# Partial sums of a two-level block multiply: gate in one ScalarE function, running sums kept in one PSUM bank

## Chip, cores and metric

The kernel runs on one core of a Trainium2 chip. The metric is the device time of one execution in microseconds (us); lower is better. The engines have these names in the profile: PE is TensorE (matrix products), PEld its loading of weights, DVE is VectorE, ACT is ScalarE, POOL is GpSimd, SP is SyncE.

## The reference

One layer of a streaming encoder on `x` of shape (1, 1024, 1024) in float32: a mixer (short convolution and forgetting attention) and then a dense SwiGLU block, each between two RMS norms. What the change touches is the first half of the SwiGLU block:

```python
def swiglu(h, w_gate_up, w_down):                  # h: (1, 1024, 1024)
    gu = jnp.einsum("bsd,df->bsf", h, w_gate_up)   # w_gate_up: (1024, 2 * 2816)
    g, u = jnp.split(gu, 2, axis=-1)
    return jnp.einsum("bsf,fd->bsd", jax.nn.silu(g) * u, w_down)
```

## The kernel before

The whole kernel is one core's program: projections, attention, merge and output projection, then the SwiGLU block with its gate_up product and its down product. All large products are done in two float32r parts: an operand is converted into a high part (`hi`, by ScalarE) and a remainder (`lo`, by VectorE), and `mm3` multiplies high by high, high by low and low by high.

**Blocks.** The hidden width 2816 is cut into 22 blocks of 128 columns (`NF`), numbered 0 to 21. A block needs its gate `g` and its `u` for 1024 rows, each held as two halves of 128 x 512. Gate and up are treated as the two block rows of a Strassen-Winograd multiply: instead of eight products there are seven, of the combinations A11, A12, S1, S2, S3, S4, A22 of weights with B11, B21, T1, T2, T3, B22, T4 of activations. One product (`prod`) is 12 matmuls of 128x128 weights with a 128x512 moving operand, accumulated in one PSUM bank; there are eight banks, handed out in turn (`bank`). The results are sums of products: gate left = A11 + A12, gate right (`c12`) = A11 + S2 + S1 + S4, up right (`c22`) = A11 + S2 + S1 + S3, up left = A11 + S2 + S3 + A22, where each name stands for its product.

**Three stretches of gate_up.** For blocks 0 to 10 (`NPRE` = 11) A11 and A12 are done earlier; their results `p1` and `g1` are kept or go through DRAM (`pre_dram`). The *rest loop* does the other five products of each of these, through `strassen(...)`, in the order S2, S1, S3, S4, A22. Block 11 (`lone`) goes through the same function with all seven. Blocks 12 to 21 go in five pairs (x, y) through `two_blocks`, where the fourth product is itself done one level deeper for the pair together (`prod2` into `zb` and into the `b3` banks).

**Order.** Instructions are listed per engine by a planner, which takes the earlier-written one first where it may choose and works with its own estimates of durations. `strict[0]` names engines on which the written order holds. It is `("tensor",)` inside `two_blocks`, so TensorE's order there is the written one; in the rest loop it is empty.

**Weights.** `prep_first` and `prep_rest` load and convert the weights of one block. The buffers rotate: four for `hi`, three for `lo`. A buffer is written again only when every reader of its earlier tile is done. In the pairs each block takes three `lo` tiles, in this order: one for A11 and A12, one (`lx`) for S2 and S3, one (`l2`) for S1 and A22. In the rest loop a block takes two, `lx` and `l2`.

```python
def hi_t():
    return wtile("hi", 4, F32R)
def lo_t():
    return wtile("lo", 3, F32R)
...
S2=(hx[:, LO], lx[:, LO]), S3=(hx[:, UP], lx[:, UP]),
S1=(h2[:, LO], l2[:, LO]), A22=(h2[:, UP], l2[:, UP]),
...
nc.tensor.matmul(ps, ah, bh, start=start, stop=False, **kw)
nc.tensor.matmul(ps, ah, bl, start=False, stop=False, **kw)
nc.tensor.matmul(ps, al, bh, start=False, stop=stop, **kw)
```

Here `a` is the weight operand and `b` the activation, so `lo` of the weights is first read by a product's third matmul and last by its twelfth.

Every engine instruction is recorded under one line (L77, the helper that passes it on), so instructions are told apart by tile: `lo<-raw,hi` is the conversion that fills an `l2` tile or that of A11 and A12, `lo<-sx,hi` that of an `lx`, `b` a PSUM bank, `c` and `um` the float32 sums in SBUF, `sgf` the sigmoid's result.

Of the kernel before, what the change touches and what calls it, by code (L numbers as in the profile page):

```python
# [12 lines left out]
AF = mybir.ActivationFunctionType  # L13
# [9 lines left out]
NC = 512  # L23
# [16 lines left out]
NPRE = 11  # L40


B11, B21, B22, T1, T2, T3, T4 = range(7)
A11, A12, A22, S2, S3, S4, S1 = range(7)
# [3 lines left out]
def block_kernel(  # L48
# [16 lines left out]
    n1, n2 = slice(0, NC), slice(NC, S)  # L65
# [3 lines left out]
    class InOrder:  # L69


        def __init__(self, name):
            self.name, self.engine = name, getattr(bass_nc, name)
# [11 lines left out]
    nc = SimpleNamespace(  # L85
        **{e: InOrder(e) for e in engines}
    )
# [7 lines left out]
    def pool(name, bufs=1, side="left", space=None):  # L95
        kw = dict(name=name, bufs=bufs)
        if space is not DRAM:
            kw["reuse_waits"] = "tile"
        if space is not None:
            kw["space"] = space  # L100
        else:
            kw["side"] = side
        stack = ExitStack()
        ctx.callback(stack.close)
        return stack.enter_context(tc.tile_pool(**kw)), stack.close
# [4 lines left out]
    def add(o, a, b):  # L110
        nc.vector.tensor_tensor(o, a, b, op=ALU.add)
# [4 lines left out]
    def mul(o, a, b):  # L116
        nc.vector.tensor_tensor(o, a, b, op=ALU.mult)
# [11 lines left out]
    def copy(o, a):  # L129
        nc.scalar.activation(o, a, AF.Copy)  # L130
# [6 lines left out]
    def mm3(ps, a, b, start, stop, **kw):  # L137

        ah, al = a
        bh, bl = b  # L140
# [4 lines that stand above are left out]
    cpool, _ = pool("const")  # L145
    stat, _ = pool("stat", 4, side="right")
    stat.tile([P, 56], F32, name="pad", bufs=1)
    dpool, _ = pool("dram", space=DRAM)
# [10 lines left out]
    pre_dram = [dpool.tile([2, P, NC], F32, name=f"pre_dram{f}") for f in range(NPRE)]  # L159
# [52 lines left out]
    def z_tile(name, dt=F32, w=S):  # L212
        return zp.tile([P, S], dt, tag="z", name=name, bufs=2)[:, :w]
# [286 lines left out]
    for st in range(2, ST):  # L500
        ops, rest = cur
# [31 lines left out]
    wpool, _ = pool("w")  # L533
# [80 lines left out]
    def bank(psp, name):  # L614
        return psp.tile([P, NC], F32, tag="mm", name=name)

    def prod(ps, w, b, first):
        (ah, al), (bh, bl) = w, b
        kw = {} if first else dict(skip_group_check=True)
        for k in range(4):  # L620
            mm3(
                ps,
                (ah[:, k, :], al[:, k, :]),
                (bh[:, k, :], bl[:, k, :]),
                first and k == 0,
                k == 3,
                **kw,
            )

    def t_(tmp, name):  # L630
        return tmp.tile([P, NC], F32, tag=name, name=name)
# [11 lines left out]
    def strassen(w, hb, psp, tmp, p1=None, mid=None):  # L643

        b1 = None
        if p1 is None:
            b1 = bank(psp, "b1")
            prod(b1, w["A11"], hb[B11], True)
            p1 = t_(tmp, "c21")
            copy(p1, b1)  # L650
        b2, b3 = bank(psp, "b2"), bank(psp, "b3")
        prod(b2, w["S2"], hb[T2], True)
        c12 = t_(tmp, "c12")
        add(c12, p1, b2)
        prod(b3, w["S1"], hb[T1], True)
        c22 = t_(tmp, "c22")
        add(c22, p1, b3)
        if b1 is not None:
            prod(b1, w["A12"], hb[B21], False)
        prod(b2, w["S3"], hb[T3], False)  # L660
        add(c22, c22, b2)
        if mid is not None:
            mid()
        prod(b3, w["S4"], hb[B22], False)
        add(c12, c12, b3)
        prod(b2, w["A22"], hb[T4], False)
        c21 = p1
        add(c21, p1, b2)
        return b1, c12, c21, c22
# [20 lines left out]
    psm, psm_close = pool("psm", 6, space=PSUM)  # L690

    def wcols(c0):
        return win[:, c0 : c0 + P]
# [352 lines left out]
    for ij, (kind, j, _, _) in enumerate(jobs):  # L1046
        work = side.pop(ij, [])

        def mid():
            for cut, _ in work:  # L1050
                pinned(cut, "vector", "scalar")
# [7 lines left out]
        if ij < 2:  # L1059
# [15 lines left out]
            w = {**w, **prep_rest(wcols(jobs[ij][3]), r1)}  # L1075
            if ij == 1:
                pairs.q.append(pairs.prep(*pairs.srcs.popleft()))
            _, c12, c21, c22 = strassen(w, h1b, psm, pp, p1, mid)
        elif ij < len(jobs) - 1:
# [3 lines left out]
            w = pairs.get()  # L1083
            if ij in (12, 13):
                cb_of(0, ij - 12)
            c11, c12, c21, c22 = strassen(w, h1b, psm, pp, None, mid)
        else:
            w = pairs.get()
# [3 lines left out]
            c11, c12, c21, c22 = last_pair(w)  # L1092
# [91 lines left out]
    was, sgs = {}, {}  # L1184
# [173 lines left out]
    for t in range(2, NU + 2):  # L1358
        turned = None
        now = groups(t) if t < NU else ([], [])  # L1360
# [17 lines left out]
        if t == NU:  # L1378
            lasts = []
            for e, engines in enumerate((("ACT", "DVE"), ("DVE", "ACT"))):  # L1380
                two = pss.tile([P, 2, NC], F32, tag="S", name="tps2", bufs=2)
# [54 lines left out]
    psm, psm_close = pool("psm2", 8, space=PSUM)  # L1436
# [175 lines left out]
    psm, psm_close = pool("psm3", 4, space=PSUM)  # L1612
# [159 lines left out]
    begun, kept = {}, {}  # L1772
# [21 lines left out]
    hb = [both(h2b11)]  # L1794
# [74 lines left out]
    psm, psm_close = pool("psm4", 8, space=PSUM)  # L1869

    hc_pool, hc_close = pool("hc")
    fp, fp_close = pool("f", 2)
# [46 lines left out]

    def gated(f, ns, g, u, t=None):  # L1920
        y = y_slot(f)[:, ns]
        t = y if t is None else t[:, ns]
        nc.scalar.activation(t, g, AF.Sigmoid)
        mul(t, t, g)
        mul(y, t, u)

    class Later:
# [87 lines left out]
    class Block:  # L2015
# [3 lines left out]
            self.f, self.w = f, w  # L2019

        def a11(self):
            self.b1, self.p1 = bank(psm, "b1"), t_(later, "c21")
            prod(self.b1, self.w["A11"], hb[B11], True)
            copy(self.p1, self.b1)

        def s2(self):
            self.b2, self.c12 = bank(psm, "b2"), t_(later, "c12")
            prod(self.b2, self.w["S2"], hb[T2], True)
            add(self.c12, self.p1, self.b2)

        def s1(self):
            self.b3, self.c22 = bank(psm, "b3"), t_(later, "c22")
            prod(self.b3, self.w["S1"], hb[T1], True)
            add(self.c22, self.p1, self.b3)

        def a12(self):
            prod(self.b1, self.w["A12"], hb[B21], False)

        def s3(self):
            prod(self.b2, self.w["S3"], hb[T3], False)  # L2040
            add(self.c22, self.c22, self.b2)

        def a22(self):
            prod(self.b2, self.w["A22"], hb[T4], False)
            add(self.p1, self.p1, self.b2)
            gated(self.f, n1, self.b1, self.p1)

        def end(self):
            gated(self.f, n2, self.c12, self.c22)

    def two_blocks(x, y, w2, more):

        tq = um[:, 7, n1]
        for step in (x.a11, x.s2, x.s1, x.a12, x.s3):
            step()
        more()
        for step in (y.a11, x.a22, y.s2, y.s1, y.a12, y.s3):
            step()
        zb_ = bank(psm, "zb")
        prod2(zb_[:, right], w2["S1"], hb2[T1], True)  # L2060
        prod2(zb_[:, left], w2["A11"], hb2[B11])
        copy(tq[:, left], zb_[:, left])
        prod2(x.b3[:, left], w2["A12"], hb2[B21])
        prod2(x.b3[:, right], w2["S4"], hb2[B22])
        add(x.c12, x.c12, x.b3)
        prod2(y.b3[:, left], w2["A22"], hb2[T4])
        add(y.c12, y.c12, y.b3)
        prod2(zb_[:, left], w2["S2"], hb2[T2])
        copy(tq[:, right], zb_[:, left])
        y.a22()  # L2070
        prod2(zb_[:, left], w2["S3"], hb2[T3])

        def ends():
            add(x.c12, x.c12, tq)
            for b in (x, y):
                add(b.c12[:, right], b.c12[:, right], zb_[:, right])
            for n in (left, right):
                add(y.c12[:, n], y.c12[:, n], zb_[:, left])
            x.end()
            y.end()  # L2080

        return ends
# [10 lines left out]
    rest = Pairs([f_src(f) for f in range(NPRE)], prep_rest_alone)  # L2093
    for _ in range(2):
        rest.more()
    for f in range(NPRE):
        if f in kept:
            p1, g1 = kept[f]
        else:
            p1 = t_(fp, "c21")  # L2100
            nc.gpsimd.dma_start(p1, pre_dram[f][0])
            g1 = z_tile("c11", w=NC)
            nc.gpsimd.dma_start(g1, pre_dram[f][1])
        _, g2, u1_, u2 = strassen(rest.get(False), hb, psm, fp, p1, rest.more)
        if f == NPRE - 1:
            lone = prep_pair(*f_src(NPRE))
        sgs = z_tile("sgf")
        gated(f, n1, g1, u1_, sgs)
        gated(f, n2, g2, u2, sgs)
        if f % 2:  # L2110
            y_sums(f // 2)
    fp_close()
    t2, t2_close = pool("t2")
    later = Later()
    even = prep_even(NPRE + 1)
    g1, g2, u1_, u2 = strassen(lone, hb, psm, later)
# [3 lines left out]
    for f in range(NPRE + 1, NF, 2):  # L2120
# [4 lines left out]
        x, y = Block(f, even), Block(f + 1, odd)  # L2125
# [158 lines left out]
    p1, c22, c11, c12 = (quarter(s_) for s_ in (4, 6, 0, 2))  # L2284
# [116 lines left out]
```

## Time and profile before

| | us |
|---|---|
| median of 3 runs | 1313.3 (1312.77 to 1314.09) |
| the profiled execution, device time | 1312.85 |
| its span in the profile | 1311.1 |
| TensorE busy | 1299.8 (99% of the span) |
| VectorE busy | 1015.2 (77%) |
| ScalarE busy | 583.5 (45%) |

The span is the time between the first and the last recorded instruction; the profiled execution's own time is 1.75 us longer. Matmul records overlap (each is about 0.39 us long, and they start about 0.23 us apart), so what a product of 12 takes is read from the starts.

### The profile page before, as it was taken

Reading aid. Unit: us, or ns where it says so; the run is one execution under the profiler, and the core shown is the slowest. Engines: PE = TensorE matmul, PEld = TensorE weight load, DVE = VectorE, ACT = ScalarE, POOL = GpSimd, SP = SyncE. Lnnn points to the kernel's source line nnn. Section 1 sums busy time; section 2 is a strip of 40 time slices with the busy share of each in tenths; the row PEclk is TensorE's granted clock in tenths of the full one; section 3 lists DMA queues with packets and bytes.
Section 4 is the critical chain, followed back from the end, with each engine's and each line's share of the span. In section 5 each row is a group of like instructions: output and inputs, shape, how many; then the busy total and the mean of one; then the engine's idle time right before and its main releaser. Section 6 shows DMA issues by size and latency. Waiting matters only on the chain.

```text
span 1311.1 us, 18310 instructions
## 1 busy us (share of the span) xinstructions
PE 1299.8 (99%) x6776; PEld 1087.3 (83%) x6776; DVE 1015.2 (77%) x1595; ACT 583.5 (45%) x935; POOL 154.9 (12%) x289
## 2 busy tenths in 40 slices
PE   9999999999999999999999999999999999999997
PEld 8988888888888888888888888888888888888886
DVE  6975979876656877588798789998887887676685
ACT  6642423243355866454576423223333334444452
POOL 0001100011112212011011021211001110000000
PEclk9999999999999999999999999999999999999999
DMA  6347667668646544589375555553223337966541
GB/s 218 114 120 225 186 173 208 173 220 231 192 137 208 161 139 138 163 311 372 139 233 191 158 169 169 183 178 104 82 98 118 106 119 276 334 245 196 156 166 65
DMA packets 207242, 235.15 MB, mean 179 GB/s; under 512 B 12064, under 2 KB 150368, under 8 KB 207152
## 3 DMA queue, kind: packets, MB, share of 16 engines
q1 hardware_dynamic: 159136, 156.08, 37.9%
q0 software_dynamic: 18832, 63.22, 13.2%
q10 hardware_dynamic: 29184, 14.68, 4.5%
q8 instruction: 53, 0.87, 0.3%
q14 instruction: 37, 0.30, 0.1%
HBM read 161.79 MB, written 72.16 MB: 178 GB/s over the span
## 4 chain that ended last, share of the span: by engine, by line
PE 93%; DVE 2%; ACT 2%; DMA 2%; issue 1%; SPq 0%; DVEq 0%; ACTq 0%
PE b L77 54%; PE pd L77 16%; PE pba L77 3%; PE pv L77 3%; PE tps L77 3%; PE po L77 3%; PE sp L77 2%; PE p L77 2%; PE pbp L77 2%; PE pbv L77 1%; PE zb L77 1%; PE ma L77 1%; PE q L77 1%; PE tp L77 1%; PE mb L77 1%
## 5 line engine op out<-in xcount | busy, mean ns | idle before, releaser
L77 PE MATMUL b<-x,hi 128*128 128x512 f32 x1088 | 335.4, 390 | 0.0
L77 PEld LDWEIGHTS b<-x,hi 128*128 128x128 f32 x1088 | 203.5, 188 | 41.6
L77 PE MATMUL b<-x,lo 128*128 128x512 f32 x544 | 212.0, 390 | 0.0
L77 DVE TENSOR_TENSOR lo<-raw,hi 128x1024 fp32r<-128x1024 f32 x90 | 108.5, 1206 | 60.1 <-PE b L77 50.1
L77 ACT ACTIVATE hi<-raw 128x1024 fp32r<-128x1024 f32 (+1 forms) x96 | 97.5, 1018 | 100.2 <-PE b L77 53.0
L77 PEld LDWEIGHTS b<-x,lo 128*128 128x128 f32 x544 | 102.1, 188 | 21.6 <-DVE lo L77 0.3
L77 DVE TENSOR_TENSOR c<-c,b 128x512 f32<-128x512 f32 x138 | 94.2, 683 | 21.2 <-PE b L77 12.9
L77 ACT ACTIVATE hi<-sx 128x1024 fp32r<-128x1024 f32 (+1 forms) x42 | 43.8, 1042 | 124.6 <-PE b L77 115.9
L77 DVE TENSOR_TENSOR lo<-sx,hi 128x1024 fp32r<-128x1024 f32 (+1 forms) x42 | 50.3, 1197 | 25.2 <-PE b L77 22.5
L77 DVE TENSOR_TENSOR sx<-raw 128x512 f32<-128x512 f32 x78 | 53.8, 689 | 20.3 <-DMA raw<-in_w_in_dram 11.2
L77 DVE TENSOR_TENSOR um<-um 128x512 f32<-128x512 f32 x93 | 62.6, 688 | 0.7
L77 PE MATMUL pd<-hi,lo 128*128 128x512 f32 x160 | 62.3, 389 | 0.0
L77 PE MATMUL pd<-hi 128*128 128x512 f32 x160 | 61.9, 390 | 0.0
L77 PE MATMUL pd<-ghi 128*128 128x512 f32 x148 | 57.7, 390 | 0.0
L77 PE MATMUL pd<-ghi,glo 128*128 128x512 f32 x148 | 57.6, 389 | 0.0
L77 PE MATMUL pd<-glo,ghi 128*128 128x512 f32 x148 | 57.6, 389 | 0.0
L77 DVE TENSOR_TENSOR um<-um,b 128x512 f32<-128x512 f32 x68 | 46.1, 683 | 9.4 <-PE b L77 8.4
L77 ACT ACTIVATE sgf<-c 128x512 f32<-128x512 f32 x20 | 12.7, 633 | 91.4 <-DVE c L77 72.4
L77 PE MATMUL b<-hT34h,lo 128*128 128x512 f32 x136 | 53.0, 389 | 0.0
L77 PE MATMUL b<-hT34h,hi 128*128 128x512 f32 x136 | 52.9, 389 | 0.0
L77 PE MATMUL b<-hT34l,hi 128*128 128x512 f32 x136 | 52.9, 389 | 0.0
L77 PE MATMUL b<-hT12h,lo 128*128 128x512 f32 x136 | 52.9, 389 | 0.0
(507 smaller groups left out, 3174.8 us busy)
## 6 DMA issues: line engine op xcount, KB each, us to landing
raw<-in_w_gate_up_dram SPq DMA_DIRECT2D x55, 512.0 KB, 4.2
raw<-in_w_in_dram SPq DMA_DIRECT2D x35, 512.0 KB, 5.0
x<-wo_dram SPq DMA_DIRECT2D x28, 512.0 KB, 7.2
a_dramS<-um POOLq DMA_DIRECT2D x44, 256.0 KB, 2.5
a_dramA<-um POOLq DMA_DIRECT2D x33, 256.0 KB, 2.6
wo_dram<-h ACTq DMA_DIRECT2D x16, 448.0 KB, 4.4
wo_dram<-l ACTq DMA_DIRECT2D x16, 448.0 KB, 6.9
sg<-sg_dram SPq DMA_DIRECT2D x28, 256.0 KB, 3.1
```

Source lines behind the costliest of these rows:

```text
L77: ins = getattr(self.engine, name)(*args, **kw)
```

## The change

`gated` uses one ScalarE function, Silu, and one VectorE multiplication where it had Sigmoid and two multiplications. In the pairs (`Block`), the sum A11, + S2, + S3, + A22 now runs in one bank (`b1`); ScalarE copies it out after A11 (`c11`), after S2 (`c12`) and after S3 (`c22`). S1 has a bank of its own (`b3`), added into `c22` once; A12 has a bank of its own, added into `c11`. The order of the products becomes A11, S1, S2, A12, S3 in place of A11, S2, S1, A12, S3, for both blocks of a pair. The rest loop gets a class `Rest`: S2 is added to `p1` by VectorE, the sum is copied back into the bank by ScalarE, and S3 and A22 accumulate on it; S2 of the next block is written ahead of A22 and S4 of this one. `strassen`, which block 11 uses, is as before apart from `gated`.

```diff
--- before.py
+++ after.py
@@ -1919,9 +1919,8 @@
 
     def gated(f, ns, g, u, t=None):
         y = y_slot(f)[:, ns]
-        t = y if t is None else t[:, ns]
-        nc.scalar.activation(t, g, AF.Sigmoid)
-        mul(t, t, g)
+        t = y if t is None else t
+        nc.scalar.activation(t, g, AF.Silu)
         mul(y, t, u)
 
     class Later:
@@ -2019,31 +2018,33 @@
             self.f, self.w = f, w
 
         def a11(self):
-            self.b1, self.p1 = bank(psm, "b1"), t_(later, "c21")
+            self.b1, self.c11 = bank(psm, "b1"), t_(later, "c21")
             prod(self.b1, self.w["A11"], hb[B11], True)
-            copy(self.p1, self.b1)
+            copy(self.c11, self.b1)
+
+        def s1(self):
+            self.b3 = bank(psm, "b3")
+            prod(self.b3, self.w["S1"], hb[T1], True)
 
         def s2(self):
-            self.b2, self.c12 = bank(psm, "b2"), t_(later, "c12")
-            prod(self.b2, self.w["S2"], hb[T2], True)
-            add(self.c12, self.p1, self.b2)
-
-        def s1(self):
-            self.b3, self.c22 = bank(psm, "b3"), t_(later, "c22")
-            prod(self.b3, self.w["S1"], hb[T1], True)
-            add(self.c22, self.p1, self.b3)
+            self.c12 = t_(later, "c12")
+            prod(self.b1, self.w["S2"], hb[T2], False)
+            copy(self.c12, self.b1)
 
         def a12(self):
-            prod(self.b1, self.w["A12"], hb[B21], False)
+            b2 = bank(psm, "b2")
+            prod(b2, self.w["A12"], hb[B21], True)
+            add(self.c11, self.c11, b2)
 
         def s3(self):
-            prod(self.b2, self.w["S3"], hb[T3], False)
-            add(self.c22, self.c22, self.b2)
+            self.c22 = t_(later, "c22")
+            prod(self.b1, self.w["S3"], hb[T3], False)
+            copy(self.c22, self.b1)
+            add(self.c22, self.c22, self.b3)
 
         def a22(self):
-            prod(self.b2, self.w["A22"], hb[T4], False)
-            add(self.p1, self.p1, self.b2)
-            gated(self.f, n1, self.b1, self.p1)
+            prod(self.b1, self.w["A22"], hb[T4], False)
+            gated(self.f, n1, self.c11, self.b1)
 
         def end(self):
             gated(self.f, n2, self.c12, self.c22)
@@ -2051,10 +2052,10 @@
     def two_blocks(x, y, w2, more):
 
         tq = um[:, 7, n1]
-        for step in (x.a11, x.s2, x.s1, x.a12, x.s3):
+        for step in (x.a11, x.s1, x.s2, x.a12, x.s3):
             step()
         more()
-        for step in (y.a11, x.a22, y.s2, y.s1, y.a12, y.s3):
+        for step in (y.a11, x.a22, y.s1, y.s2, y.a12, y.s3):
             step()
         zb_ = bank(psm, "zb")
         prod2(zb_[:, right], w2["S1"], hb2[T1], True)
@@ -2093,20 +2094,48 @@
     rest = Pairs([f_src(f) for f in range(NPRE)], prep_rest_alone)
     for _ in range(2):
         rest.more()
+
+    class Rest:
+
+
+        def __init__(self, f):
+            self.f, self.w = f, rest.get(False)
+            if f in kept:
+                self.p1, self.g1 = kept[f]
+            else:
+                self.p1 = t_(fp, "c21")
+                nc.gpsimd.dma_start(self.p1, pre_dram[f][0])
+                self.g1 = z_tile("c11", w=NC)
+                nc.gpsimd.dma_start(self.g1, pre_dram[f][1])
+            self.b2, self.c12 = bank(psm, "b2"), t_(fp, "c12")
+            prod(self.b2, self.w["S2"], hb[T2], True)
+            add(self.c12, self.p1, self.b2)
+            copy(self.b2, self.c12)
+
+        def two(self):
+            self.b3, self.c22 = bank(psm, "b3"), t_(fp, "c22")
+            prod(self.b3, self.w["S1"], hb[T1], True)
+            prod(self.b2, self.w["S3"], hb[T3], False)
+            copy(self.c22, self.b2)
+            add(self.c22, self.c22, self.b3)
+
+        def end(self):
+            prod(self.b2, self.w["A22"], hb[T4], False)
+            prod(self.b3, self.w["S4"], hb[B22], False)
+            gated(self.f, n1, self.g1, self.b2, self.g1)
+            add(self.c12, self.c12, self.b3)
+            gated(self.f, n2, self.c12, self.c22, self.c12)
+
+    now = Rest(0)
     for f in range(NPRE):
-        if f in kept:
-            p1, g1 = kept[f]
+        now.two()
+        rest.more()
+        if f + 1 < NPRE:
+            after = Rest(f + 1)
         else:
-            p1 = t_(fp, "c21")
-            nc.gpsimd.dma_start(p1, pre_dram[f][0])
-            g1 = z_tile("c11", w=NC)
-            nc.gpsimd.dma_start(g1, pre_dram[f][1])
-        _, g2, u1_, u2 = strassen(rest.get(False), hb, psm, fp, p1, rest.more)
-        if f == NPRE - 1:
             lone = prep_pair(*f_src(NPRE))
-        sgs = z_tile("sgf")
-        gated(f, n1, g1, u1_, sgs)
-        gated(f, n2, g2, u2, sgs)
+        now.end()
+        now = after
         if f % 2:
             y_sums(f // 2)
     fp_close()
```

## Rows read from the trace of the kernel before

**Rows 1.** The page: span, then busy time, share and instructions of each engine.

```profile
span 1311.1 us, 18310 instructions
...
PE 1299.8 (99%) x6776; PEld 1087.3 (83%) x6776; DVE 1015.2 (77%) x1595; ACT 583.5 (45%) x935; POOL 154.9 (12%) x289
```

**Rows 2.** Chain that ended last: start us, length us, what.

```profile
694.81 240.74 PE b L77 x1062
...
973.26 1.43 PE zb L77 x12
...
1010.98 1.43 PE zb L77 x12
```

**Rows 3.** Waits of TensorE, whole run: us in total, times, longest.

```profile
PE spin L77 <- POOL ident masks.py:199: 1.5, 1, 1.5
...
PE p L77 <- ACT c L77: 0.4, 1, 0.4
PE b L77 <- ACT c L77: 0.3, 1, 0.3
```

**Rows 4.** Stretches: busy us of each engine, granted clock, DMA share, GB/s.

```profile
830.20:892.00 61.80, 61.80 (x274) 51.19 (x273) 58.93 (x89) 20.14 (x27) 11.39 (x21) 1.00 0.52 163
...
1018.50:1056.20 37.70, 37.70 (x189) 32.05 (x188) 32.41 (x51) 12.73 (x19) 3.78 (x7) 1.00 0.32 105
1056.20:1093.90 37.70, 37.70 (x188) 32.05 (x187) 26.25 (x41) 11.89 (x18) 3.79 (x7) 1.00 0.47 161
```

**Rows 5.** Timeline of TensorE, second iteration: start us, length us, operation, tiles.

```profile
943.15 0.40 PE L77 MATMUL b<-x,hi 128*128 128x512 f32 x1
...
961.99 0.39 PE L77 MATMUL b<-x,lo 128*128 128x512 f32 x1
962.22 0.62 PE L77 MATMUL b<-x,hi 128*128 128x512 f32 x2
962.67 0.39 PE L77 MATMUL b<-x,lo 128*128 128x512 f32 x1
```

**Rows 6.** Timeline of VectorE, first, second and fifth iteration; idle before in brackets.

```profile
924.70 1.23 DVE L77 TENSOR_TENSOR lo<-raw,hi 128x1024 fp32r<-128x1024 f32 x1 [0.21 <-PE b L77]
...
962.42 1.23 DVE L77 TENSOR_TENSOR lo<-raw,hi 128x1024 fp32r<-128x1024 f32 x1 [0.20 <-PE b L77]
...
1075.58 1.23 DVE L77 TENSOR_TENSOR lo<-raw,hi 128x1024 fp32r<-128x1024 f32 x1 [0.20 <-PE b L77]
```

**Rows 7.** Timeline around 320: one TensorE wait for a ScalarE copy.

```profile
319.90 0.57 ACT L77 ACTIVATE c<-b 128x512 f32<-128x512 f32 x1
...
320.52 0.50 PE L77 MATMUL b<-hB21h,hi 128*128 128x512 f32 x1 [0.28 <-ACT c L77]
...
320.86 0.40 PE L77 MATMUL b<-hB21l,hi 128*128 128x512 f32 x1
```

**Rows 8.** Timeline of ScalarE, end of the first iteration and in the second.

```profile
935.40 1.06 ACT L77 ACTIVATE hi<-raw 128x1024 fp32r<-128x1024 f32 x1 [1.18 <-issue]
...
946.10 0.60 ACT L77 ACTIVATE um<-b 128x512 f32<-128x512 f32 x1 [0.64 <-PE b L77]
...
956.80 1.06 ACT L77 ACTIVATE hi<-raw 128x1024 fp32r<-128x1024 f32 x1 [1.16 <-issue]
```

**Rows 9.** Timeline of TensorE, end of the first iteration.

```profile
935.38 0.28 PE L77 MATMUL zb<-hch,s4h 128*128 128x256 f32 x1
...
938.25 0.28 PE L77 MATMUL b<-t22h,s4h 128*128 128x256 f32 x1
```

**Rows 10.** Timeline of VectorE, end of the first iteration.

```profile
936.72 0.68 DVE L77 TENSOR_TENSOR um<-um,b 128x512 f32<-128x512 f32 x1
938.00 0.69 DVE L77 TENSOR_TENSOR sx<-raw 128x512 f32<-128x512 f32 x1 [0.60 <-DMA raw<-in_w_gate_up_dram]
```

**Rows 11.** Groups, 736 to 886 (the rest loop): busy us, mean ns, idle before.

```profile
L77 DVE TENSOR_TENSOR c<-c,b 128x512 f32<-128x512 f32 x48 | 32.7, 682 | 0.3 <-PE b L77 0.3
...
L77 ACT ACTIVATE sgf<-c 128x512 f32<-128x512 f32 x20 | 12.7, 633 | 91.4 <-DVE c L77 72.4 <-DVE um L77 19.0
```

## Prediction

> **What bounds the kernel.** I read the page first, then the chain that ended last, then TensorE's waits, then stretches, and at last timelines of the pairs.
>
> The page shows TensorE busy for 1299.8 of 1311.1 us [rows 1]. Matmul records overlap, so a busy share alone does not say that the rate is full. The chain says more: from 694.81 us to the end of gate_up it is TensorE all the way, with no other engine in between [rows 2]. Its first piece there is 1062 matmuls that take 240.74 us, 0.2267 us each. A product of 12 takes 2.72 us. One iteration of the pairs lasts 37.72 us: the zb pieces return at 973.26 and again at 1010.98, that far apart, and 12 products of 2.72 plus seven short ones of 0.72 make 37.7. So nothing is idle there. TensorE's longest wait for another engine in the whole run is 1.5 us, at the start, and its two waits for a ScalarE copy are 0.4 and 0.3 us [rows 3]; none of them is on the chain after 694.81.
>
> Could a less loaded VectorE let TensorE run faster? The stretches answer. In the rest loop VectorE is busy for 58.93 of 61.80 us, in the fifth iteration of the pairs for only 26.25 of 37.70, against 32.41 in the fourth. TensorE's matmul count in those two iterations is the same, 188 or 189 in 37.70 us, at a granted clock of 1.00, the 2.4 GHz level [rows 4]. VectorE's load does not set TensorE's rate. So the change cannot gain from the work that it takes off VectorE. It can only lose, where it makes TensorE wait.
>
> The Trainium skill ("Trainium Kernel Development and Optimization", Best Practices) says to judge the distance to the limit by the weight loads' busy share, not by the matmuls'. Here that share is 83%, which by the rule would leave headroom; the equal counts at unequal VectorE loads say that this change does not reach it.
>
> **Part 1: engine work moved.** A VectorE pass over 128x512 takes 0.68 us [rows 11]. In the rest loop a block had five additions and four multiplications, now three and two: four fewer, times 11. In the pairs eight passes become four, times 10. Block 11 saves two. That is 86 passes, 59 us of VectorE. ScalarE gains two copies a block, 42 over 21 blocks, at 0.60 us [rows 8] 25 us. No row shows Silu; its nearest row is the sigmoid of the same shape, 0.633 us [rows 11], and even twice that would lie beside matmuls, as ScalarE is busy for 12.73 of 37.70 us [rows 4]. TensorE's matmul count does not change. Value of this part: 0. It cannot be below 0, since no TensorE wait stands in this stretch to be won; above 0 it can only come through the handovers of part 3, which are costed there.
>
> **Part 2: S1 moved ahead of S2 in the pairs.** This is the step that costs. With three lo tiles a block and three buffers, the second block's `l2` (operand of its S1 and A22) always gets the buffer that held the first block's `l2`. It can be written only when x's A22, its last reader, is done. Before, TensorE then did y's S2 while VectorE filled it; y's S1 came 2.72 us later. Now y's S1 follows directly on x's A22.
>
> The second iteration starts at 943.15, and x's A22 is its seventh product: 943.15 + 7 x 2.72 = 962.19 is its end. The rows fit: its last matmul starts at 961.99 and ends at 962.38, and the next product starts at 962.22 [rows 5]. VectorE's `lo<-raw,hi` starts at 962.42, waiting for that matmul, and lasts 1.23 us to 963.65 [rows 6]. The same conversion of 1.22 to 1.23 us, with a wait of 0.20 or 0.21 us for TensorE, stands in all five iterations, 37.72 us apart (three are shown); before, all of it lay under y's S2.
>
> After the change the third matmul of y's S1, the first to read `lo`, would be due at 962.67 [rows 5] but cannot start before 963.65. How late TensorE starts after such a wait is seen at 320: the copy ends at 320.47, the matmul starts at 320.52, and the next follows after 0.34 in place of 0.23 us [rows 7]. So 963.70 - 962.67 + 0.11 = 1.14 us a pair, 5.7 us for five. From below it is 0.98 (no latency), 4.9 us. From above VectorE has one 0.68 us addition in hand when the buffer comes free: 1.82, 9.1 us. I take 5.7, since VectorE stood waiting at that point all five times. x's own `l2` is safe: it waits for y's A22 of the iteration before, and a zb piece of 0.72 and A11 of 2.72 lie between that and x's S1.
>
> **Part 3: sums kept in one bank.** Each copy now has to leave the bank before TensorE may add to it again, and one product lies between. A copy costs from matmul end to restart: x's A11 of the second iteration is copied at 946.10 for 0.60 us [rows 8], when the next matmul would have started at 943.15 + 2.72 = 945.87. With 0.05 us to restart that is 0.88, plus the 0.11 slow start 0.99 us if nothing covered it. A product covers 2.72. The tight places:
>
> - x's S3, then x's A22, with y's A11 between. ScalarE begins a 1.06 us conversion at 956.80, just as x's S3 ends [rows 8]; a copy behind it runs from about 957.77 to 958.37, 1.1 us before x's A22 is due at 959.47. Hidden.
> - y's S3, then the short product into y's `b3`. `b3` must be added into `c22` first, since that product writes into it. The matmul that does so starts at 938.25, 2.87 us after the zb pieces start at 935.38 [rows 9]. ScalarE has a conversion from 935.40 [rows 8], so the copy runs about 936.37 to 936.97, and the addition (0.68) to 937.70. VectorE is free then: its addition of 936.72 ends at 937.40, the next item waits for a transfer until 938.00 [rows 10]. If that addition too is still there, it ends at 938.1. Hidden by 0.1 to 0.5 us; if one more pass stands in the way, 0.6 us a pair, 3 us for five.
> - The rest loop: S3, copy, A22, with the next block's S2 between: hidden as the first. At its last block no S2 is left to cover. There the handover costs 0 (if the planner puts in block 11's A11, which has its operands) to 0.99. I take 0.4, the size of the two waits for a copy that the trace has [rows 3].
> - S2, VectorE's addition, copy back, then S3: three products of 8.2 us lie between, except at block 0 with one. 0.68 + 0.60 and latencies fit into 2.72.
>
> The Trainium skill ("Perfetto Trace Analysis", Matmuls) speaks against this part: independent matmul groups should rotate through banks, so that the evacuation of one overlaps the next group. By it the handovers would be paid; the rows above show another product in between at each of them but one.
>
> **Sum.** 1312.85 (the profiled execution) + 5.7 + 0.4 = 1318.95 us. That execution lies 0.45 below the median of the runs, so I forecast 1319.4 against 1313.3, 0.46% slower. What the measurement can tell from no change is about 0.2%, 2.6 us, so slower begins at 1315.9.
>
> **Rivals.**
>
> - *More handovers miss.* An engine works its list in order; ScalarE stood 72.4 us at sigmoids that waited for VectorE in the rest loop [rows 11], and a copy behind such a wait is late. Against it: each item has a product to hide in. Price: part 2 plus 0.6 to 1.0 us at each pair, 3 to 5 us, 1322.4 to 1324.4; with the rest loop's 11 blocks at 0.5 us on top up to 1330.
> - *Not slower: the buffer comes free earlier.* If x's A22 and y's S1 do not share a buffer, VectorE converts ahead and the swap is free. It decides at 1.14 us: the conversion must start that much before x's A22 ends. It would give 1313.3 (with the 0.4 still 1313.7). Against it: in all five iterations the conversion starts 0.04 us after x's A22 ends, having waited for it [rows 5, 6].
> - *Faster: VectorE was holding TensorE after all.* It would have to win 2.6 us. The waits on record lie outside the changed part; if both copy waits [rows 3] went away, that is 0.7 us: 1312.6.
>
> **Chances and range.** The forecast's case 0.62, more handovers 0.22, buffer free 0.12, faster 0.04. The likeliest case alone runs from 1317.5 to 1322.4. For 8 in 10 the range leaves out most of the two last cases and the top of the second: 1315.5 to 1326. Slower by over 0.2%: the first two, 0.84; within 0.2%: 0.13; faster by over 0.2%: 0.03, a part of the last case.
>
> **What would show it.** In the changed kernel's trace: five TensorE gaps of about 1.1 us, each two matmuls into y's S1, behind `lo<-raw,hi`; an iteration of 38.9 us in place of 37.7; the rest loop still 13.6 us a block; VectorE some 59 us less busy. Waits of TensorE for ScalarE copies or for VectorE additions would be the first rival; an iteration of 37.7 us the second. I am wrong if those five gaps are not there, or if they are and the time does not grow, which would need TensorE time given back elsewhere.

## The result, and the profile after

The changed kernel takes 1319.9 us (median of 5, 1318.73 to 1321.43) against 1313.3 us (1311.38 to 1314.09). The ratio is 1.0051, interval 1.0037 to 1.0065: slower by about 0.5%. The forecast was 1319.4. Of all the executions behind the medians in this document, one, of run 9, took 1440.13 us at a granted clock of 0.85 (0.998 or 0.999 in every other); it counts in that run's median and not in its ratio.

The page of the changed kernel, beside [rows 1]:

```profile
span 1318.2 us, 18276 instructions
...
PE 1302.3 (99%) x6776; PEld 1087.7 (83%) x6776; DVE 966.5 (73%) x1509; ACT 608.4 (46%) x977; POOL 154.9 (12%) x289
```

The same 6776 matmuls, 86 VectorE instructions fewer, 42 ScalarE instructions more, and a span longer by 7.1 us. TensorE's busy share is 99% in both. Shares do not show where the time went. TensorE's waits from 690 us to the end of gate_up do (us in total, times, longest):

```profile
PE b L77 <- DVE lo L77: 4.3, 5, 0.9
PE b L77 <- ACT b L77: 0.7, 1, 0.7
PE tp L77 <- DVE keep L77: 0.5, 1, 0.5
```

Five waits for a `lo` conversion by VectorE and one for a ScalarE copy into a bank are new. The third kind stood before too, at the same place ahead of the changed part, with 0.2 us. TensorE's timeline shows one of the five (start us, length us; idle before in brackets), beside [rows 5]:

```profile
964.48 0.39 PE L77 MATMUL b<-x,lo 128*128 128x512 f32 x1
964.71 0.61 PE L77 MATMUL b<-x,hi 128*128 128x512 f32 x2
966.19 0.50 PE L77 MATMUL b<-x,lo 128*128 128x512 f32 x1 [0.86 <-DVE lo L77]
966.52 0.63 PE L77 MATMUL b<-x,hi 128*128 128x512 f32 x2
```

VectorE's timeline at the same place, beside [rows 6]:

```profile
964.28 0.42 DVE L77 TENSOR_TENSOR l2b<-raw,l2b 128x256 fp32r<-128x256 f32 x1
964.91 1.22 DVE L77 TENSOR_TENSOR lo<-raw,hi 128x1024 fp32r<-128x1024 f32 x1 [0.21 <-PE b L77]
```

x's A22 has its twelfth matmul at 964.48, ending at 964.87. VectorE's conversion starts at 964.91 and ends at 966.13. y's S1 runs its first two matmuls at once, and its third, the first to read `lo`, starts at 966.19. Due it was at 964.71 + 2 x 0.227 = 965.16. So it is 1.03 us late, and the next one follows after 0.33 us in place of 0.23. The bracket (0.86) understates this, since it counts only from the end of the matmul record before.

The chain that ended last, beside [rows 2], gives the cost of a pair and of the whole:

```profile
927.30 10.73 PE b L77 x46
...
966.19 10.74 PE b L77 x46
...
1005.09 10.76 PE b L77 x46
...
1101.42 209.77 PE pd L77 x924
```

A pair lasts 966.19 - 927.30 = 38.89 us in place of 37.72: 1.17 us more, 5.9 for five. The down product starts at 1101.42; before it started at 1094.20, and 694.81 to 694.92 at the head of the stretch is a shift of 0.1. So of 7.2 us the pairs have 5.9. Of the rest, 1.2 lie between the head of the stretch and the pairs; about 1 us of that is block 0 of the rest loop:

```profile
739.46 0.39 PE L77 MATMUL b<-x,lo 128*128 128x512 f32 x1
...
742.18 0.39 PE L77 MATMUL b<-x,lo 128*128 128x512 f32 x1
743.26 0.73 PE L77 MATMUL b<-x,hi 128*128 128x512 f32 x2 [0.69 <-ACT b L77]
```

VectorE's timeline there, then ScalarE's:

```profile
735.05 0.69 DVE L77 TENSOR_TENSOR sx<-raw 128x512 f32<-128x512 f32 x1 [2.26 <-DMA raw<-in_w_gate_up_dram]
...
739.34 1.23 DVE L77 TENSOR_TENSOR lo<-sx,hi 128x1024 fp32r<-128x1024 f32 x1 [0.41 <-ACT hi L77]
741.28 0.69 DVE L77 TENSOR_TENSOR s4l<-s,s4h 128x512 fp32r<-128x512 f32 x1 [0.72 <-ACT s4h L77]
741.89 0.68 DVE L77 TENSOR_TENSOR c<-um,b 128x512 f32<-128x512 f32 x1
```

```profile
742.61 0.60 ACT L77 ACTIVATE b<-c 128x512 f32<-128x512 f32 x1 [0.83 <-DVE c L77]
```

Block 0's S3 was due at 742.41. S1 takes the 2.72 us before that, so the last matmul of S2 is at the latest the one at 739.46, whose record ends at 739.85. The addition that reads S2 began only at 741.89. VectorE had stood idle for 2.26 us until a transfer of weights landed; then came the preparation of those weights, `lo<-sx,hi` and `s4l<-s,s4h` last, with another 0.72 us of idle for ScalarE's `s4h`; and only then, in VectorE's list, the addition.

The stretches, beside [rows 4], show the relief that bought nothing (busy us of TensorE, its weight loads, VectorE, ScalarE):

```profile
830.20:892.00 61.80, 61.80 (x273) 50.97 (x272) 48.32 (x70) 23.27 (x33) 10.84 (x20) 1.00 0.51 161
```

In this stretch of the rest loop VectorE fell from 58.93 to 48.32 of 61.80 us, and TensorE did 273 matmuls there, against 274 before.

### The profile page after: what moved, and what is told of

Read it like the earlier page. It is cut to its first block, busy times and chain, and to the rows that moved or that the text cites. A ratio compares the mean times of both kernels' runs of the same rounds, so it can differ in the third digit from the quotient of the medians.

```text
span 1318.2 us, 18276 instructions
## 1 busy us (share of the span) xinstructions
PE 1302.3 (99%) x6776; PEld 1087.7 (83%) x6776; DVE 966.5 (73%) x1509; ACT 608.4 (46%) x977; POOL 154.9 (12%) x289
## 4 chain that ended last, share of the span: by engine, by line
PE 91%; DVE 3%; ACT 2%; DMA 2%; issue 1%; DVEq 0%; POOL 0%; ACTq 0%; POOLq 0%
PE b L77 52%; PE pd L77 16%; PE pba L77 3%; PE pv L77 3%; PE tps L77 3%; PE po L77 3%; PE sp L77 2%; PE p L77 2%; PE pbp L77 2%; PE pbv L77 1%; PE zb L77 1%; DMA raw<-in_w_gate_up_dram 1%; DVE lo L77 1%; PE ma L77 1%; PE q L77 1%
## 5 line engine op out<-in xcount | busy, mean ns | idle before, releaser
L77 DVE TENSOR_TENSOR c<-c,b 128x512 f32<-128x512 f32 x120 | 81.7, 682 | 30.8 <-PE b L77 22.6
L77 PE MATMUL b<-hT12h,hi 128*128 128x512 f32 x136 | 52.9, 389 | 0.0
L77 PE MATMUL b<-hT12l,hi 128*128 128x512 f32 x136 | 52.9, 389 | 0.0
L77 ACT ACTIVATE pt<-pt,nm 128x1024 f32<-128x1024 f32 (+7 forms) x62 | 47.0, 760 | 8.8 <-DVE nm L77 8.5
```

The source lines that it names most:

```text
L77: ins = getattr(self.engine, name)(*args, **kw)
```

## Experiments

The theory from the prediction: y's S1, directly behind x's A22, waits for a conversion into the buffer that x's A22 was reading (*buffer theory*). Rivals: it is the handovers of the one bank that cost, or the order of the products as such. Medians of 5 or 11 runs; each kernel was timed beside the kernel before, whose median there was 1312.6 to 1312.8 us, and the ratio is to that.

**1. The changed kernel with y's order put back.**

```diff
-        for step in (y.a11, x.a22, y.s1, y.s2, y.a12, y.s3):
+        for step in (y.a11, x.a22, y.s2, y.s1, y.a12, y.s3):
```

> The changed kernel with only the order of the second block of a pair put back (A22 of x, then y's S2, then y's S1). Buffer theory (y's S1 waits for the conversion into the buffer that x's A22 held): the five gaps of 0.86 us go, the iteration falls from 38.9 to 37.7 us, the time from 1319.9 by 5 x 1.18 = 5.9 to about 1314.0. Handover theory (the copies out of the one bank are what TensorE pays for): the copies are all still there, so the time stays near 1319.9. A mixed outcome: the gaps move to waits for ScalarE copies, 1316 to 1319.

Measured: 1313.74 us, ratio 1.0009 (1.0000 to 1.0018). Behind 694 us one line of TensorE waits is left:

```profile
PE b L77 <- ACT b L77: 0.5, 1, 0.5
```

All five gaps are gone with all handovers in place; block 0's wait (0.5) stays.

**2. The kernel before with y's order changed, and nothing else.** The same line, the other way round.

> The kernel before with only that one order changed: y's S1 ahead of y's S2, sigmoid, five additions and three banks as before. Buffer theory: five gaps of about 0.86 us at the third matmul of y's S1, 1313.3 + 5.9 = 1319.2. Handover theory: nothing was handed over differently, 1313.3.

Measured: 1318.5 us, ratio 1.0045 (1.0032 to 1.0058). Its waits in the stretch are one line:

```profile
PE b L77 <- DVE lo L77: 4.3, 5, 0.9
```

The reordering alone makes the same five gaps, and nothing of the new sums is needed for them. With run 1 this settles the handovers: they are neither needed for the loss nor enough for it.

**3. Half the conversion.** The changed kernel; for y, `l2` is converted in two passes, the half that S1 reads first.

```diff
+        if keep == "there":
+            copy(h2, r2)
+            for half in (LO, UP):
+                sub(l2[:, half], r2[:, half], f32(h2[:, half]))
+        else:
+            split(h2, l2, r2)
```

> The changed kernel, with the conversion of l2 of y written in two passes of 128x512 (0.69 us each), the half that S1 reads first. Buffer theory, as a dose: TensorE is let go after one pass of 0.69 in place of 1.22 us, so each gap shrinks by about 0.54 us, from 1.18 to about 0.62 a pair: 1319.9 - 2.7 = 1317.2. If the gap does not depend on the length of the conversion: 1319.9.

Measured: 1318.12 us, ratio 1.0042 (1.0029 to 1.0054). TensorE's timeline and the chain of this kernel:

```profile
966.04 0.50 PE L77 MATMUL b<-x,lo 128*128 128x512 f32 x1 [0.33 <-DVE lo L77]
```

```profile
966.04 10.73 PE b L77 x46
...
1004.40 10.74 PE b L77 x46
```

The gap shrinks by 0.53 us, a pair takes 38.36 in place of 38.89, as expected: the wait shrinks by what the conversion is shorter. The median fell by only 1.8 of the expected 2.7 us, and the profiled span by 1.7. In the profile the loss is ahead of the changed part: from the start of the chain's TensorE stretch to the down product it is 403.84 us in place of 406.50, 2.66 less, but that stretch begins 0.9 us later.

**4. The same order, another buffer.** A fourth `lo` buffer would be the plainest test; it does not fit (16 KB a partition, where 12 are left), so no time shows it. A first try with three took y's buffer for S1 and A22 earlier in the text without writing it earlier.

```diff
+        l2 = lo_t() if keep == "there" else None
         hx, lx = hi_t(), lo_t()
         split(hx, lx, sx)
-        h2, l2 = hi_t(), lo_t()
+        h2, l2 = hi_t(), lo_t() if l2 is None else l2
```

> The changed kernel, order as changed, same three lo buffers, but the second block of a pair takes its lo tile for S1 and A22 before the one for S2 and S3, so that it follows in the buffer of x's S2 and S3, free after x's S3, and the one for S2 and S3 follows in that of x's A22, with y's S1 of 2.72 us to cover the conversion. Buffer theory: the five gaps go although the order of products stays as changed, 1319.9 - 5.9 = 1314.0, like the run with the old order (1313.7). Order theory (S1 directly behind A22 is itself what costs): 1319.9.

Measured: 1320.42 us, ratio 1.0060 (1.0047 to 1.0072), the same five gaps. VectorE's list in the changed stretch came out the same as in the changed kernel: buffers follow the order of the first writes. So the run says nothing on the question: it repeats the changed kernel, 0.5 us from its first measurement. The second try writes the conversion earlier:

```diff
+        if keep == "there":
+            h2, l2 = hi_t(), lo_t()
+            split(h2, l2, r2)
         hx, lx = hi_t(), lo_t()
         split(hx, lx, sx)
-        h2, l2 = hi_t(), lo_t()
-        split(h2, l2, r2)
+        if keep != "there":
+            h2, l2 = hi_t(), lo_t()
+            split(h2, l2, r2)
```

> The changed kernel, order of products as changed, same three lo buffers; for the second block of a pair the conversion for S1 and A22 is written ahead of that for S2 and S3, so that it is the one that follows in the buffer of x's S2 and S3 (free after x's S3), and the conversion for S2 and S3 waits for x's A22 under y's S1 of 2.72 us. The run before this one with that aim assigned the buffers as before and was a repeat. Buffer theory: the five gaps go with the order of products unchanged, 1319.9 - 5.9 = 1314.0. Order theory: 1319.9.

Measured: 1314.27 us, ratio 1.0013 (1.0004 to 1.0021). VectorE's timeline of this kernel:

```profile
959.11 1.22 DVE L77 TENSOR_TENSOR lo<-raw,hi 128x1024 fp32r<-128x1024 f32 x1
...
964.47 1.23 DVE L77 TENSOR_TENSOR lo<-sx,hi 128x1024 fp32r<-128x1024 f32 x1 [0.21 <-PE b L77]
```

`lo<-raw,hi` now stands 5 us earlier, and it is the conversion for S2 and S3 that waits for x's A22, under y's S1. No TensorE wait is left in the pairs, though S1 still follows directly on A22. It was the shared buffer, not the order as such. The one wait left is block 0's:

```profile
PE b L77 <- ACT b L77: 1.5, 1, 1.5
```

**5. An uncovered handover.** The changed kernel with the old order in x as well: x's S2 then follows on A11 in the same bank with no product between.

```diff
-        for step in (x.a11, x.s1, x.s2, x.a12, x.s3):
+        for step in (x.a11, x.s2, x.s1, x.a12, x.s3):
...
-        for step in (y.a11, x.a22, y.s1, y.s2, y.a12, y.s3):
+        for step in (y.a11, x.a22, y.s2, y.s1, y.a12, y.s3):
```

> The changed kernel with the old order in both blocks of a pair, the sums still in one bank: x's S2 now follows directly on x's A11, so the copy out of the bank has no product to hide under, while y still has x's A22 there. My price for an uncovered handover, 0.99 us, five times: 1313.7 + 5.0 = 1318.7, as five TensorE waits for a ScalarE copy ahead of x's S2. If handovers cost nothing even when uncovered: 1313.7. If ScalarE is behind with other work there: 1320 or more.

Measured: 1319.1 us, ratio 1.0049 (1.0036 to 1.0061). ScalarE's and then TensorE's timeline of this kernel:

```profile
948.30 0.60 ACT L77 ACTIVATE um<-b 128x512 f32<-128x512 f32 x1 [0.64 <-PE b L77]
```

```profile
947.88 0.39 PE L77 MATMUL b<-x,lo 128*128 128x512 f32 x1
948.95 0.73 PE L77 MATMUL b<-x,hi 128*128 128x512 f32 x2 [0.69 <-ACT um L77]
```

Five such waits; a pair takes 987.65 - 948.95 = 38.70 us between them, 0.98 more than 37.72, where 0.99 was worked out. So a running sum in one bank does need another product between A11 and S2; in x, S1 does this. In y, x's A22 stands there already; swapping y too is what cost.

**6. The rest loop and the gate alone.** The pairs' class and order from the kernel before.

> The changed rest loop and the Silu gate, with the pairs as in the kernel before. Buffer theory: no gap in the pairs, and only block 0's wait for the copy back (0.69 us of idle, about 0.9 in all): about 1313.7 to 1314.2. If the rest loop carried part of the loss beyond that: 1315 or more. If moving work off VectorE gained anything: below 1313.

Measured: 1318.18 us, ratio 1.0044 (1.0031 to 1.0056). This missed: 4 us more than expected, in pairs whose text is that of the kernel before but for the gate.

```profile
PE b L77 <- DVE um L77: 2.7, 5, 0.5
```

Five waits for a VectorE addition; block 0's wait is absent here (why is shown behind run 9). Which of the two edits brings them was the next question.

**7. The gate alone.** The kernel before with Silu.

```diff
-        nc.scalar.activation(t, g, AF.Sigmoid)
-        mul(t, t, g)
+        nc.scalar.activation(t, g, AF.Silu)
```

> The kernel before with Silu and one multiplication in place of sigmoid and two, nothing else. By my prediction's part 1: 1313.3, no wait, some 27 us less VectorE work. By what the run with only the rest loop changed showed in its untouched pairs (VectorE's addition into c22 came behind other work in its list, TensorE waited 0.54 us for it five times, 0.84 a pair): if the shorter gate alone makes the planner list VectorE's work so, 1313.3 + 4.2 = 1317.5; if it takes the changed rest loop, 1313.3.

Measured: 1317.48 us, ratio 1.0043 (1.0029 to 1.0057), and the same five waits. VectorE's timeline of this kernel, then TensorE's:

```profile
957.75 1.23 DVE L77 TENSOR_TENSOR lo<-sx,hi 128x1024 fp32r<-128x1024 f32 x1
958.89 0.42 DVE L77 TENSOR_TENSOR s<-raw,s 128x256 f32<-128x256 f32 x1
959.22 0.69 DVE L77 TENSOR_TENSOR s4l<-raw,s4h 128x512 fp32r<-128x512 f32 x1
959.83 0.42 DVE L77 TENSOR_TENSOR s<-s 128x256 f32<-128x256 f32 x1
960.16 0.68 DVE L77 TENSOR_TENSOR um<-um,b 128x512 f32<-128x512 f32 x1
```

```profile
960.90 0.73 PE L77 MATMUL b<-x,hi 128*128 128x512 f32 x2 [0.54 <-DVE um L77]
```

`um<-um,b` is the addition of x's S3 into `c22`. In the kernel before x's A22 accumulates in the bank that this addition reads, so it must end first; only y's A11, 2.72 us, lies between. In the list of the kernel before it stood two items behind the conversion `lo<-sx,hi`:

```profile
957.07 1.22 DVE L77 TENSOR_TENSOR lo<-sx,hi 128x1024 fp32r<-128x1024 f32 x1
958.20 0.42 DVE L77 TENSOR_TENSOR raw<-raw 128x256 f32<-128x256 f32 x1
958.53 0.68 DVE L77 TENSOR_TENSOR um<-um,b 128x512 f32<-128x512 f32 x1
```

There it ended at 959.21, 0.29 us before x's A22 started:

```profile
959.50 0.61 PE L77 MATMUL b<-x,hi 128*128 128x512 f32 x2
```

With 20 multiplications fewer in the pairs the addition stands two items later in VectorE's list, and VectorE, with less to do, delivers it later. A pair takes 960.90 - 922.34 = 38.56 us from wait to wait, 0.84 more than 37.72, so 4.2 for five; the median lies 4.8 above that of the kernel before beside it (1312.64).

**8. That addition put first.** Run 6 with the addition after S3 given priority.

```diff
-            add(self.c22, self.c22, self.b2)
+            ahead(lambda: add(self.c22, self.c22, self.b2), 400)
```

> The run with only the rest loop and the gate changed (1318.2), with one more edit: VectorE's addition of the bank into c22 after S3 is given priority in the planner, so that it is listed ahead of the conversion for S2 and S3. List theory: the five waits of 0.54 us go, 1318.2 - 4.2 = 1314.0, the level of the kernel before within 1 us. If the waits come from something else in the rest loop: 1318.2.

Measured: 1313.49 us, ratio 1.0008 (1.0000 to 1.0017). The five waits are gone; block 0's is back (1.7 in the profile). It was the place in VectorE's list: with Silu and the changed rest loop both kept, moving the addition forward is enough.

**9. Both waits of the changed kernel taken away.** y's order as before, and no copy back in block 0.

```diff
-        for step in (y.a11, x.a22, y.s1, y.s2, y.a12, y.s3):
+        for step in (y.a11, x.a22, y.s2, y.s1, y.a12, y.s3):
...
-            copy(self.b2, self.c12)
+            if f:
+                copy(self.b2, self.c12)
...
+            if not self.f:
+                add(self.c22, self.c22, self.p1)
...
+            u = self.b2
+            if not self.f:
+                add(self.p1, self.p1, self.b2)
+                u = self.p1
-            gated(self.f, n1, self.g1, self.b2, self.g1)
+            gated(self.f, n1, self.g1, u, self.g1)
```

> The changed kernel with y's order put back and, in block 0 of the rest loop only, no copy back into the bank (two more additions on VectorE there). Both waits known in the changed kernel are then gone: TensorE waits for nothing in the whole stretch, 1312.8 to 1313.3, equal to the kernel before, with some 49 us less VectorE work. If VectorE's load had held TensorE anywhere: clearly below 1312.

Measured: 1313.29 us, ratio 1.0002 (0.9993 to 1.0012). No TensorE wait is listed behind 694 us. VectorE is busy for 967.9 us of the whole run, 47 us less than in the kernel before, and the time is the same. No version beat the kernel before.

**Block 0's wait, read across the runs.** Its size changes from run to run, and the traces show with what. In VectorE's list the preparation of weights described above stands ahead of the addition, and its first item waits for a transfer. Run 8, VectorE, then TensorE:

```profile
735.12 0.69 DVE L77 TENSOR_TENSOR sx<-raw 128x512 f32<-128x512 f32 x1 [3.23 <-DMA raw<-in_w_gate_up_dram]
```

```profile
743.33 0.73 PE L77 MATMUL b<-x,hi 128*128 128x512 f32 x2 [1.67 <-ACT b L77]
```

Run 6, VectorE:

```profile
734.78 0.69 DVE L77 TENSOR_TENSOR sx<-raw 128x512 f32<-128x512 f32 x1 [1.25 <-DMA raw<-in_w_gate_up_dram]
```

| | VectorE idle for the transfer, us | TensorE's wait, us |
|---|---|---|
| run 6 | 1.25 | none |
| run 1 | 2.11 | 0.55 |
| changed kernel | 2.26 | 0.69 |
| run 4, second try | 3.03 | 1.47 |
| run 8 | 3.23 | 1.67 |

Where TensorE waits, its wait is VectorE's less 1.56 or 1.57 us; runs 3 and 5 and the first try of run 4 fit as well. So a late transfer, handed on through VectorE's list, is what block 0 pays for. In the kernel before VectorE had the same idle time there, 2.23 us, at no cost, since nothing was copied back into the bank. What makes the transfer land earlier or later was not traced.

## Why the prediction was right, point by point

- **What bounds the kernel.** Right. With every TensorE wait of the changed stretch taken away and 47 us of VectorE work less, the time is that of the kernel before (run 9). The Trainium skill's rule on the weight loads' share ("Trainium Kernel Development and Optimization", Best Practices) does not help here: the share is 83% before, after and in run 9, and no lighter VectorE raised it.
- **Part 2, S1 ahead of S2.** Right in place, cause and size: 1.14 us a pair was worked out, 1.17 measured. It was shown by the reordering alone (run 2), by its reversal (run 1), by half the conversion (run 3) and by another buffer with the order kept (run 4).
- **Part 3, handovers.** Right in the pairs: no wait there, and 0.98 us when uncovered (run 5), where 0.99 was the price. The Trainium skill's rule on rotating banks ("Perfetto Trace Analysis", Matmuls) holds as a warning: the evacuation has to be overlapped by something, and in the pairs the product between did it as well as another bank. Wrong at the rest loop's two ends. The last block, for which I put 0.4, had no wait. Block 0, which I let fit into 2.72, had one that cost about 1 us: S2 had ended by 739.85 us, but VectorE's addition stood until 741.89 behind the preparation of weights, which had waited for a transfer. I had added up durations and not looked at what stood ahead in VectorE's list. The two errors partly cancel, by luck, and leave about 0.6 us too little in the sum.
- **Part 1, work moved.** The counts were exact (86 and 42 instructions) and ScalarE's 25 us measured 24.9. VectorE's 59 us measured 48.7: passes back to back start 0.60 us apart though each record is 0.68 long (957.89 and 958.49 in the changed kernel), so a busy time counts less than the sum of the records; 86 passes of 0.60 would be 51.6. That the part costs 0 held for this change, but not for the reason given, that it could cost only through the new handovers. Alone, with none of them, the shorter gate costs 4.2 us in the pairs (run 7), through a wait on VectorE that stood 0.29 us from showing. In the changed kernel that place is gone, because x's A22 waits there for ScalarE's copy.
- **The rivals.** "More handovers miss" did not occur in the pairs and once in the rest loop, at block 0; runs 6 and 7 are its mechanism on VectorE. "The buffer comes free earlier" is what run 4 made true, with the time foreseen within 1 us. "Faster" is excluded by run 9.
- **The range.** The lower end of the likeliest case, 1317.5, does not follow from its terms: 1312.85 + 4.9 is 1317.75, and both ends leave out the 0.45 that the forecast adds. The measured time lies well inside either way.

What stays open: why the planner lists the addition later when the gate is shorter, what sets the landing of the transfer that block 0 waits for, and the last 0.2 to 0.3 us of the 1.2 between the head of the stretch and the pairs.

## What to carry to other kernels

When one engine has no gap, taking work off another gains nothing, and the only question about an edit is which wait it can add: for each product moved, look up which buffers its operands follow in, and which reader has to be done first. Covers are counted in products: a conversion of 1.23 us or a copy of 0.60 cost nothing here behind one product of 2.72 when its engine could start at once, and 1.17 or 0.98 us without one. Whether the engine can start at once is read from what stands ahead in its list, transfers included: block 0 had its product of 2.72 and waited all the same. And read the margin of each cover in the trace of before: one of 0.29 us can be lost to any edit that shifts another engine's list, even one that shortens it.

## What the runs showed of the hardware

After a wait TensorE starts 0.05 to 0.06 us behind the releasing operation's end, its first matmul record is 0.50 long in place of 0.39, and the next starts 0.33 us later in place of 0.23; so a gap costs about 0.3 us more than the idle time that the profile puts in its bracket. Four sizes show it, bracket against growth of a pair: 0.86 and 1.17 us (changed kernel), 0.69 and 0.98 (run 5), 0.54 and 0.84 (run 7), 0.33 and 0.64 (run 3).
